# A fused attention and state-space layer: splits one tile per dense slice, a skip added in PSUM, a third result buffer

## The chip, the cores and the metric

One NeuronCore of a Trainium2 chip runs the whole layer as one program. The metric is the device time of one execution in microseconds (us). Engines are named as the profile names them: PE multiplies matrices (PEld loads its weights), DVE, ACT and POOL are the vector, scalar and general engines, and SP issues DMA transfers. PE writes its results to PSUM, in banks of 128 x 512 float32; the other tiles lie in SBUF.

## The reference

One layer over 1024 positions of 1024 channels, in float32. A combined projection feeds a sparse attention and a state-space (SSD) mixer; both are projected back, gated, merged, and followed by a SwiGLU block. What the change touches is the mixer's scan, its gate and norm, and the projections of both branches:

```python
    CB = jnp.einsum('bclgn,bcsgn->bcgls', Cc, Bc)
    y_diag = jnp.einsum('bcgls,bcgrls,bcsgrp->bclgrp', CB, Lmat, X)
    ...
    y_off = jnp.einsum('bclgn,bcgrpn,bcgrl->bclgrp', Cc, prev, jnp.exp(a_cum))
    y = (y_diag + y_off).reshape(Bsz, L, SSD_HEADS, SSD_HEADDIM) + d_skip[:, None] * xh
    y = y.reshape(Bsz, L, D_INNER)
    return rmsnorm(y * jax.nn.silu(z), ssd_norm)
```

`d_skip * xh` is D's skip. `Lmat` holds the exponentials of the decay between two positions of a chunk.

## The kernel before

Activations lie transposed, channels on partitions. Dense matrices keep float32 accuracy by three matmuls on two halves: a tile is split into a rounded "hi" (written by ACT) and the rest "lo" (written by DVE or POOL). For weights these are `whi` and `wlo` (L158, L159), for the attention's output `ath` and `atl` (L1299, L1303), for the mixer's output `yh` and `yw` (L1277, L1278).

The mixer works in 32 units, unit n = 4g + c for 8 head groups g and 4 chunks c of 256 positions. A unit has two generators. `ssd_in` loads `ld` (L1163, L1164) and the decay table `al` (L1169). ACT makes relu and exponentials of two tiles, the late part `M` and `al` (L1174 to L1176); PE multiplies B and C into `pcb`; DVE masks it to `cbm` (L1182) and multiplies it into `M` and `al` (L1184); X and the state's factors follow. `ssd_out` runs one unit later: PE's `pyd` (L1224, the part inside the chunk, which needs `al`) and `pyo` (L1234, the part from the state, absent for c = 0). DVE multiplies the decay `d_ea`, which was loaded into the result tile (L1218), by pyo (L1236), adds pyd (L1237), and adds D's skip for two tiles (L1241). For c = 0 ACT copies pyd in place of the first two (L1239). POOL multiplies by the gate z (L1243), SP stores to `d_y` (L1244), and ACT squares the result into `ysqt` (L1247) for the norm's sums on DVE (L1254).

Between these steps PE runs slices of dense work, six matmuls each, from the generator `beside`: the last gate projections (`pw`, `gate_run`), and the attention's output projection (`poa`, `poa_run`). The same generator splits what they need: `at_split` splits four tiles of the attention's output at once, and `y_load` loads and splits the first twelve tiles of the mixer's y for the projection `pos` (L1647), which follows the mixer.

The order on PE is the order in which the program is written (`in_order`). The order on ACT, DVE, POOL and SP is set by a scheduler from its own simulated times, when the program is built; added "behind" dependencies keep an instruction after another of the same engine. `exps[0]` names the two exponentials of the unit last begun, and `ysqt` is kept behind one of them. Each engine takes its queue strictly in order. DMAs from SP go round eight lanes, whose semaphores are DMAHW0 to DMAHW7, and each waits for the one eight before it.

The result tile, with z in one half and y in the other, comes from `vt` (one buffer) for every third unit and otherwise from the ring "R", which also serves `ld` and `al`. A load into a tile waits until its last use is over, for a result tile the store to `d_y`.

Of the kernel before, what the change touches and what calls it, by code (L numbers as in the profile page):

```python
# [10 lines left out]
F32 = mybir.dt.float32  # L11
F32R = mybir.dt.float32r
BF = mybir.dt.bfloat16
AF = mybir.ActivationFunctionType
OP = mybir.AluOpType
AX = mybir.AxisListType

P = 128
# [3 lines left out]
NT = L // P  # L22
# [17 lines left out]
POA_BOTH = 5  # L40
# [3 lines left out]
SK = 8  # L44
# [25 lines left out]
def build(tc, a, dbg=None, stop=99, slots=None):  # L70
    nc = tc.nc
    V, S, G, T, SP = nc.vector, nc.scalar, nc.gpsimd, nc.tensor, nc.sync
# [5 lines left out]
    wp = ctx.enter_context(tc.tile_pool(name="wp", bufs=2))  # L78
    vp = ctx.enter_context(tc.tile_pool(name="vp", bufs=1))
    H_ = Arena(ctx, tc, "H", n_slots["H"], 512)  # L80
    Q = Arena(ctx, tc, "Q", n_slots["Q"], 512)
    R = Arena(ctx, tc, "R", n_slots["R"], 1024)
# [105 lines left out]
    def col(name, j=0, n=1):  # L188
        o, _ = COLS[name]
        return vec[:, o + j:o + j + n]  # L190
# [6 lines left out]
    dsk = con.tile([P, 16], F32, name="dsk")  # L197
# [957 lines left out]
    exps = [None]  # L1155
# [51 lines left out]
    def ssd_out(c, g, z):  # L1207
        hs = slice(4 * g, 4 * g + 4)
        cl = slice(QC * c, QC * c + QC)
        X, M, xs, CT = z["X"], z["M"], z["xs"], z["bc"][:, 1]  # L1210
        st = state[:, g]
        zy = (vp.tile([P, NT, P], F32, name="vt", bufs=1).rearrange("p (j x) n -> p j (x n)", j=4) if (4 * g + c) % 3 == 0
              else R("zy", (P, 4, 256)))
        zc, yt = zy[:, 0:2], zy[:, 2:4]
        SP.dma_start(zc, d_z[2 * g:2 * g + 2].rearrange("j p l -> p j l")[:, :, cl])
        if c:
            for e in range(2):
                SP.dma_start(yt[64 * e:64 * e + 64],  # L1218
                             d_ea[c, hs].rearrange("(j e) l -> e j l", e=2)[e:e + 1].to_broadcast([64, 2, QC]))
        pyd = bank("pyd")  # L1220
        for j in range(2):
            for e in range(2):
                o = pyd[64 * e:64 * e + 64, 256 * j:256 * j + 256]
                T.matmul(o, X[:, 0, 2 * j + e], M[j][:, e], start=True, stop=False, skip_group_check=True)  # L1224
                T.matmul(o[:, 128:256], X[:, 1, 2 * j + e], M[2][:, 2 * j + e], start=False, stop=True, skip_group_check=True)
        if c < NCH - 1:
            pst = bank("pst")
            for t in range(2):
                T.matmul(pst[:, 0:256], z["bn"][:, t], z["Xd"][:, t].rearrange("p h n -> p (h n)"), start=t == 0, stop=t == 1)
        yield  # L1230
        if c:
            pyo = bank("pyo")
            for j in range(2):
                T.matmul(pyo[:, 256 * j:256 * j + 256], st[:, 128 * j:128 * j + 128], CT, start=True, stop=True)  # L1234
            ytf = yt.rearrange("p j l -> p (j l)")
            V.tensor_tensor(ytf, ytf, pyo, op=OP.mult)  # L1236
            V.tensor_tensor(ytf, ytf, pyd, op=OP.add)  # L1237
        else:
            S.activation(yt.rearrange("p j l -> p (j l)"), pyd, AF.Copy)  # L1239
        for j in range(2):  # L1240
            V.scalar_tensor_tensor(yt[:, j, :], xs[:, j], dsk[:, 2 * g + j:2 * g + j + 1], yt[:, j, :],  # L1241
                                   op0=OP.mult, op1=OP.add)
        G.tensor_tensor(yt, yt, zc, op=OP.mult)  # L1243
        SP.dma_start(d_y[2 * g:2 * g + 2].rearrange("j p l -> p j l")[:, :, cl], yt)  # L1244
        yield
        sq = Q("ysqt", (P, 2, 256))
        tc.add_manual_dep(S.activation(sq, yt, AF.Square).ins, exps[0][1], mybir.DependencyInfo(  # L1247
            mybir.DependencyClass.NoSync, mybir.DependencyReason.DATA), reason="behind")
        for j in range(2):
            ya_ = ysq[c // 2][:, QC * (c % 2):QC * (c % 2) + QC]  # L1250
            if g == 0 and j == 0:
                S.activation(ya_, sq[:, j], AF.Copy)
            else:
                V.tensor_tensor(ya_, ya_, sq[:, j], op=OP.add)  # L1254
        if c == 0:
            S.activation(st, pst[:, 0:256], AF.Copy)
        elif c < NCH - 1:
            G.tensor_tensor(st.rearrange("p (h n) -> p h n", h=4), st.rearrange("p (h n) -> p h n", h=4),
                            cdec[:, c, hs, None].to_broadcast([P, 4, 64]), op=OP.mult)
            V.tensor_tensor(st, st, pst[:, 0:256], op=OP.add)  # L1260
        yield
# [3 lines left out]
    def y_raw(k, b):  # L1265
        t = EV("yl")
        SP.dma_start(t, d_y[k][:, half(b)])
        return t

    def y_parts(i, j, src, where, scale=None, eng=V):  # L1270

        hi, lo = where("yh", dt=F32R), where("yw", dt=F32R)
        if scale is None:
            ins = S.activation(hi, src, AF.Copy)
            eng.tensor_tensor(lo, src, f(hi), op=OP.subtract)
        else:
            ins = S.activation(hi, src, AF.Copy, scale=scale)  # L1277
            V.scalar_tensor_tensor(lo, src, scale, f(hi), op0=OP.mult, op1=OP.subtract)  # L1278
        YO[i][j] = hi, lo
        return ins.ins  # L1280

    def y_load(ks, places):
        for k in ks:
            y_parts(1 + k // SK, k % SK, y_raw(k, 0), places(k), col("ssd_norm", k))

    def beside():

        AT = [([None, None], [None, None]) for _ in range(KT)]

        def at_load(b, ks, where):  # L1290
            raws = [EV("atl") for k in ks]
            for t, k in zip(raws, ks):
                SP.dma_start(t, d_att[k][:, half(b)])
            return b, ks, where, raws

        def at_split(b, ks, where, raws):
            for t, k in zip(raws, ks):
                hi, lo = where("ath", dt=F32R), where("atl", dt=F32R)
                i = S.activation(hi, t, AF.Copy).ins  # L1299
                for j in (ahead[0], *exps[0]):  # L1300
                    tc.add_manual_dep(i, j, mybir.DependencyInfo(
                        mybir.DependencyClass.NoSync, mybir.DependencyReason.DATA), reason="behind")
                (G if k % 2 else V).tensor_tensor(lo, t, f(hi), op=OP.subtract)  # L1303
                AT[k][0][b], AT[k][1][b] = hi, lo

        ahead = [None]

        def anchor(ins):
            ahead[0] = ins.ins.name

        def gate_run(t, b, w):
            p = bank_d("pw")
            yield from dense_steps(p, b, w, Hs)
            g = EV("g")
            anchor(S.activation(g, p, AF.Tanh, scale=0.5))
            SP.dma_start(d_gb[t][:, half(b)], g)
            yield

        def poa_run(t, b, w):
            ya = EV("ya")  # L1320
            SP.dma_start(ya, d_sga[t][:, half(b)])
            p = bank_d("poa")
            yield from dense_steps(p, b, w, AT)
            i = V.scalar_tensor_tensor(ya, ya, 1.0, p, op0=OP.add, op1=OP.mult)
            SP.dma_start(d_ya[t][:, half(b)], ya)
            yield

        def two_tiles(src, ts):
            W.plan(col_tile(src[ts[0]]) + col_tile(src[ts[1]])[:1])
            return [wpieces(ks8), [(W.next(), 0, ks8[:4]), (small_weights(src[ts[1]][:, 4:8]), 0, ks8[4:])]]  # L1330

        for t in range(6):
            yield from gate_steps(57 + t, d_gb[t])
        ld = at_load(0, range(AT_IN_Q), Q)
        w = two_tiles([a["w_in"][57 + t] for t in range(8)], (6, 7))
        yield from gate_run(6, 0, w[0])
        at_split(*ld)
        ld = at_load(0, range(AT_IN_Q, KT), H_)
        yield from gate_run(7, 0, w[1])
        at_split(*ld)  # L1340
        ld = at_load(1, range(4), H_)
        yield from gate_run(6, 1, w[0])
        at_split(*ld)
        ld = at_load(1, range(4, KT), H_)
        yield from gate_run(7, 1, w[1])
        w = two_tiles(a["w_o_attn"], (0, 1))
        yield from poa_run(0, 0, w[0])
        at_split(*ld)
        yield from poa_run(1, 0, w[1])
        for i in range(2):  # L1350
            yield from poa_run(i, 1, w[i])
        for ts, bs in [((t,), BS) for t in range(2, POA_BOTH)] + [(range(POA_BOTH, 8), (b,)) for b in BS]:
            for t in ts:
                W.plan(col_tile(a["w_o_attn"][t]))
                w = wpieces(ks8)
                for b in bs:
                    yield from poa_run(t, b, w)
            if bs == (0,):
                y_load(range(12), y_place)

    def y_place(k):
        return Q if k in Y_IN_Q else H_
# [801 lines left out]
```

## Time and profile before

| | us |
|---|---|
| median of three runs | 2359.83 (2356.86 to 2364.58) |
| profiled execution | 2361.0 |
| its span, first to last instruction | 2359.2 |
| mean granted clock of PE | 0.992 of full speed |
| PE busy | 2308.6 |
| DVE, ACT, POOL busy | 1658.4, 1220.9, 988.0 |
| the mixer's units | about 1118 to 1450 |
| step to the projection of y | about 1440 to 1500 |

Times within the span count from its start. Rows of the timeline give start, duration, engine, line, operation, out<-in, and in brackets how long the engine was idle before and which instruction ended that. Rows of waits give the total, the number of times and the longest. The granted clock is the share of full speed that PE was allowed.

### The profile page before, as it was taken

How to read it: one execution, taken by the hardware profiler on the slowest of the kernel's cores; microseconds unless marked ns; L12 is line 12 of the kernel's file. 1: busy time of each engine (PE TensorE's matmuls, PEld its weight loads, DVE VectorE, ACT ScalarE, POOL GpSimd, SP SyncE). 2: the span in 40 equal slices, each digit the busy share in tenths (PEclk: the TensorE clock that was granted, in tenths of full speed). 3: DMA queues.
4: the chain of work that ended last, by engine and by line, in shares of the span. 5: the costliest groups of instructions: out<-in, count | busy, mean ns of one | idle time of the engine just before them, and what ended most of it. 6: DMA issues, size and time to landing. Idle time of an engine off the chain costs nothing.

```text
span 2359.2 us, 35056 instructions
## 1 busy us (share of the span) xinstructions
PE 2308.6 (98%) x11736; PEld 1889.5 (80%) x11736; DVE 1658.4 (70%) x3185; ACT 1220.9 (52%) x2362; POOL 988.0 (42%) x787
## 2 busy tenths in 40 slices
PE   8999999999999999999999989999999999999997
PEld 5878888888888888887887777878788888888887
DVE  5467887499676767776678769865868776646675
ACT  4346666467645555556667565444555222235542
POOL 1435552522245656554445443000113445554556
PEclk8999999999999999999999999999999999999999
DMA  7137542622233433344679888864483444428664
GB/s 271 63 122 246 191 175 94 192 94 94 103 110 118 140 128 128 126 139 154 215 238 291 250 272 277 278 202 143 144 277 138 151 149 154 158 96 285 209 189 168
DMA packets 251716, 411.27 MB, mean 174 GB/s; under 512 B 25568, under 2 KB 93328, under 8 KB 251536
## 3 DMA queue, kind: packets, MB, share of 16 engines
q1 hardware_dynamic: 238288, 387.48, 49.2%
q10 hardware_dynamic: 13248, 21.56, 3.0%
q8 instruction: 92, 1.51, 0.3%
q14 instruction: 88, 0.72, 0.1%
HBM read 304.84 MB, written 107.24 MB: 175 GB/s over the span
## 4 chain that ended last, share of the span: by engine, by line
PE 74%; DVE 11%; DMA 7%; ACT 3%; issue 2%; POOL 1%; SPq 1%; DVEq 0%; ACTq 0%; POOLq 0%
PE p L1723 18%; PE pw L234 14%; PE pfo L1988 8%; PE pw L244 7%; PE plg L847 4%; PE pos L1647 3%; PE pot L1435 3%; PE prel L648 3%; PE pt L880 3%; PE po L896 3%; DVE junk L702 2%; PE puq L234 2%; DMA yl<-d_y 2%; PE poa L244 2%; DMA d_y<-zy 1%
## 5 line engine op out<-in xcount | busy, mean ns | idle before, releaser
L159 POOL TENSOR_TENSOR wlo<-wraw,whi 128x512 fp32r<-128x512 f32 x152 | 210.4, 1385 | 334.0 <-ACT whi L158 307.7
L1723 PE MATMUL p<-xh,wr 128*128 128x512 f32 x880 | 271.8, 389 | 0.0
L158 ACT ACTIVATE whi<-wraw 128x512 fp32r<-128x512 f32 x238 | 149.1, 627 | 214.0 <-issue 57.4
L1723 PEld LDWEIGHTS p<-xh,wr 128*128 128x128 f32 x880 | 165.2, 188 | 34.3
L1717 POOL TENSOR_TENSOR wr<-a,wr 128x512 fp32r<-128x512 f32 x82 | 115.2, 1413 | 134.0 <-ACT wr L1716 97.8
L1723 PE MATMUL p<-xl,wr 128*128 128x512 f32 x440 | 171.2, 389 | 0.0
L255 POOL TENSOR_TENSOR fwl<-fw,fwh 128x512 fp32r<-128x512 f32 (+1 forms) x78 | 106.7, 1377 | 104.0 <-ACT fwh L254 78.9
L1716 ACT ACTIVATE wr<-a 128x512 fp32r<-128x512 f32 x107 | 66.6, 629 | 127.5 <-PE p L1723 90.7
L859 ACT ACTIVATE lg<-lg,mx 128x256 f32<-128x256 f32 (+7 forms) x128 | 99.1, 774 | 58.3 <-DVE mx L856 50.8
L273 POOL TENSOR_TENSOR r<-v,nhalf 128x4 f32<-128x4 f32 (+1 forms) x17 | 20.0, 1178 | 260.7 <-DVE v L271 260.7
L654 DVE SCALAR_TENSOR_TENSOR acc<-rel,widx,acc 128x384 f32<-128x384 f32 (+2 forms) x90 | 102.9, 1168 | 15.8 <-ACT rel L649 15.6
L329 POOL TENSOR_TENSOR adaw<-adaw,cs 128x512 f32<-128x512 f32 x64 | 68.3, 1068 | 103.2 <-DMA adaw<-ada_w 93.1
L1723 PE MATMUL p<-h2h,wr 128*128 128x512 f32 x352 | 110.0, 390 | 0.0
L704 ACT ACTIVATE junk<-acc,cand__2216 128x1024 bf16<-128x1024 f32 (+2 forms) x96 | 86.2, 898 | 39.6 <-DVE cand__2216 L747 30.7
L649 ACT ACTIVATE rel<-prel 128x512 f32<-128x512 f32 (+3 forms) x160 | 76.9, 523 | 46.5 <-PE prel L648 43.3
L1723 PEld LDWEIGHTS p<-xl,wr 128*128 128x128 f32 x440 | 82.6, 188 | 17.1
L1647 PE MATMUL pos<-yh,wlo 128*128 128x512 f32 x224 | 87.9, 392 | 3.7 <-DVE wlo L159 2.3
L702 DVE TENSOR_SCALAR_CACHE_REDUCE junk<-acc,cand__2225 128x896 bf16<-128x896 f32 (+2 forms) x96 | 88.5, 922 | 1.5
L856 DVE CUSTOM_DVE_ANT_0 lg<-plg,nm 128x256 f32<-128x256 f32 (+1 forms) x128 | 51.5, 404 | 52.8 <-PE plg L847 52.1
L1647 PE MATMUL pos<-yh,whi 128*128 128x512 f32 x224 | 88.0, 393 | 0.5 <-ACT whi L158 0.4
L1717 POOL TENSOR_TENSOR wr<-s,wr 128x512 fp32r<-128x512 f32 x40 | 56.1, 1402 | 76.4 <-ACT wr L1716 69.2
L1647 PE MATMUL pos<-yw,whi 128*128 128x512 f32 x224 | 87.3, 390 | 0.0
(693 smaller groups left out, 7446.2 us busy)
## 6 DMA issues: line engine op xcount, KB each, us to landing
wraw<-w_in SPq DMA_DIRECT2D x129, 256.0 KB, 2.7
a<-w_ffn_in SPq DMA_DIRECT2D x122, 256.0 KB, 3.3
al<-d_a SPq DMA_DIRECT2D x88, 256.0 KB, 4.2
yl<-d_y SPq DMA_DIRECT2D x72, 256.0 KB, 4.6
adaw<-ada_w SPq DMA_DIRECT2D x64, 256.0 KB, 3.0
al<-d_ac SPq DMA_DIRECT2D x32, 512.0 KB, 5.2
d_a<-g SPq DMA_DIRECT2D x42, 256.0 KB, 2.4
ada<-ada_p SPq DMA_DIRECT2D x16, 512.0 KB, 7.6
```

What stands on the lines that cost most here:

```text
L158: self.hi = behind(S.activation(hi[:, :kt], raw[:, :kt], AF.Copy))
L159: self.lo = behind(self.eng[len(self.tiles) % len(self.eng)].tensor_tensor(lo[:, :kt], raw[:, :kt], f(hi[:, :kt]), op=OP.subtract))
L234: T.matmul(o, wt[:, k0 + i, :], xs[k][xi][b][:, sl], start=pi == 0 and i == 0 and wt is hi and xi == 0, stop=pi == len(pcs) - 1 and i == l ...
L244: T.matmul(o, wt[:, k0 + j, :], xs[k][xi][b], start=i == 0, stop=i == 23)
L255: (lo_eng or V).tensor_tensor(lo, src, f(hi), op=OP.subtract)
L654: V.scalar_tensor_tensor(acc[i][:, 0:n], rel[:, 0:n], ws, acc[i][:, 0:n], op0=OP.mult, op1=OP.add)
L702: V.tensor_scalar(jk, y, a_, 0.0, op0=op, op1=OP.add, accum_out=o)
L859: S.activation(lg[:, 0:n], lg[:, 0:n], AF.Exp, scale=-1.0, bias=m, accum_out=rr[:, 2 * t + hh:2 * t + hh + 1])
L1647: T.matmul(p, w[k // 4][wi][:, k % 4], YO[i][k][xi], start=start and k == 0 and n == 0, stop=k == SK - 1 and n == 2, skip_group_check=True)
L1717: parts_last[0] = parts_eng[0].tensor_tensor(w[:, 1], src, f(w[:, 0]), op=OP.subtract).ins.name
L1723: T.matmul(p, w[:, wi, i], X[x][i][xi], start=start and i == 0 and k == 0, stop=i == 3 and k == 2, skip_group_check=True)
L1988: T.matmul(p, w[wi][:, k - k0], xs[k][xi][:, sl], start=start and k == 0 and i == 0, stop=k == KH - 1 and i == 2, skip_group_check=True)
```

## The change

Four edits. (1) D's skip is added to pyd in PSUM, as soon as pyd is there, and after pyo only two instructions remain on DVE; for c = 0 the skip writes the result tile from pyd itself, and ACT's copy goes. (2) A third result buffer: where n % 3 is 1, z and y are two tiles of an earlier stage's tag `adaw`, and the ring "R" is left out. (3) `at_split` returns jobs, one tile each, which `along` runs one per dense slice. (4) `y_load` too returns one job per tile, loads up to two tiles ahead, and its `yh` is kept behind the exponentials of the unit last begun; the twelve jobs run along the last six `poa_run`s (2, 1, 1, then 4, 2, 2), where they stood together after the third of these.

```diff
-        zy = (vp.tile([P, NT, P], F32, name="vt", bufs=1).rearrange("p (j x) n -> p j (x n)", j=4) if (4 * g + c) % 3 == 0
-              else R("zy", (P, 4, 256)))
-        zc, yt = zy[:, 0:2], zy[:, 2:4]
+        if (4 * g + c) % 3 == 1:
+            zcf, ytf = (wp.tile([P, 4, P], F32, name="zy", tag="adaw", bufs=2).rearrange("p k m -> p (k m)") for _ in range(2))
+        else:
+            zy = (vp.tile([P, NT, P], F32, name="vt", bufs=1).rearrange("p k m -> p (k m)") if (4 * g + c) % 3 == 0 else R("zy"))
+            zcf, ytf = zy[:, 0:512], zy[:, 512:1024]
+        zc, yt = (x.rearrange("p (j l) -> p j l", j=2) for x in (zcf, ytf))
...
-            ytf = yt.rearrange("p j l -> p (j l)")
             V.tensor_tensor(ytf, ytf, pyo, op=OP.mult)
+        for j in range(2):
+            py = pyd[:, 256 * j:256 * j + 256]
+            V.scalar_tensor_tensor(py if c else yt[:, j], xs[:, j], dsk[:, 2 * g + j:2 * g + j + 1], py,
+                                   op0=OP.mult, op1=OP.add)
+        if c:
             V.tensor_tensor(ytf, ytf, pyd, op=OP.add)
-        else:
-            S.activation(yt.rearrange("p j l -> p (j l)"), pyd, AF.Copy)
-        for j in range(2):
-            V.scalar_tensor_tensor(yt[:, j, :], xs[:, j], dsk[:, 2 * g + j:2 * g + j + 1], yt[:, j, :],
-                                   op0=OP.mult, op1=OP.add)
...
-    def y_load(ks, places):
-        for k in ks:
-            y_parts(1 + k // SK, k % SK, y_raw(k, 0), places(k), col("ssd_norm", k))
+    def y_load(ks, places, tie):
+
+        raws = {}
+
+        def load(k):
+            if k in ks:
+                raws[k] = y_raw(k, 0)
+
+        def one(k):
+            for x in range(k, k + 3):
+                if x not in raws:
+                    load(x)
+            tie(y_parts(1 + k // SK, k % SK, raws[k], places(k), col("ssd_norm", k)))
+
+        return [lambda k=k: one(k) for k in ks]
...
+            return [lambda t=t, k=k: one(t, k) for t, k in zip(raws, ks)]
+
+        def behind_exps(i):
+            for j in (ahead[0], *exps[0]):
+                tc.add_manual_dep(i, j, mybir.DependencyInfo(
+                    mybir.DependencyClass.NoSync, mybir.DependencyReason.DATA), reason="behind")
+
+        def along(run, jobs):
+
+            jobs = list(jobs)
+            for _ in run:
+                if jobs:
+                    jobs.pop(0)()
+                yield
+            for job in jobs:
+                job()
...
-        at_split(*ld)
+        jobs = at_split(*ld)
         ld = at_load(0, range(AT_IN_Q, KT), H_)
-        yield from gate_run(7, 0, w[1])
+        yield from along(gate_run(7, 0, w[1]), jobs)
...
+        y_jobs = y_load(range(12), y_place, behind_exps)
...
-                    yield from poa_run(t, b, w)
-            if bs == (0,):
-                y_load(range(12), y_place)
+                    n = len(bs) == 1 and ((2, 1, 1), (4, 2, 2))[b][t - POA_BOTH]
+                    yield from along(poa_run(t, b, w), [y_jobs.pop(0) for _ in range(n)])
```

The order on PE is the same in both kernels. On the other engines it differs from about 1100 us of the profile until about 1550, where both run alike again. Three places follow. In the rows, the number behind a name tells buffers apart, "waits" lists the semaphores that an instruction waits for, and their suffix is a mere number.

First ACT at unit 24 before the change. Its tiles are `al_13922` and `M_13924`; `al_14014` belongs to unit 25.

```order
L1201 ACTIVATE bn_13967<-pbn_13964 128x256
L1175 ACTIVATE al_13922<-al_13922,acum_941 128x256 x4
L1176 ACTIVATE M_13924<-M_13924 128x512
L1277 ACTIVATE yh_14732<-yl_14730,vec_87 128x512
L1176 ACTIVATE al_13922<-al_13922 128x1024
L158 ACTIVATE whi_14241<-wraw_14240 128x512
L1247 ACTIVATE ysqt_14007<-zy_13977 128x512
```

The first split of y stands between the two exponentials of the unit. After the change, with unit 24's tiles `al_13924` and `M_13926`:

```order
L1201 ACTIVATE bn_13969<-pbn_13966 128x256
L1175 ACTIVATE al_13924<-al_13924,acum_941 128x256 x4
L1176 ACTIVATE M_13926<-M_13926 128x512
L1176 ACTIVATE al_13924<-al_13924 128x1024
L158 ACTIVATE whi_14243<-wraw_14242 128x512
L1249 ACTIVATE ysqt_14009<-zy_13979 128x512
```

The split has left this place: the first one now follows the exponentials of unit 29.

Second, ACT at unit 17 before, with the tiles `al_13230` and `M_13232`; `M_13336` is unit 18's.

```order
L1176 ACTIVATE M_13232<-M_13232 128x512
L174 ACTIVATE uh_13382<-uraw_13381 128x512
L1315 ACTIVATE g_13353<-pw_13267 128x512
L1247 ACTIVATE ysqt_13326<-zy_13301 128x512
L1174 ACTIVATE M_13336<-al_13334,acum_941 128x128 x4
L1176 ACTIVATE al_13230<-al_13230 128x1024
L1299 ACTIVATE ath_13243<-atl_13144 128x512
```

Four instructions, relu of the next unit among them, stand between the exponentials. After the change, with `al_13231` and `M_13233`:

```order
L1176 ACTIVATE M_13233<-M_13233 128x512
L1258 ACTIVATE state_11603<-pst_13306 128x256
L1176 ACTIVATE al_13231<-al_13231 128x1024
L1314 ACTIVATE ath_13259<-atl_13129 128x512
L174 ACTIVATE uh_13383<-uraw_13382 128x512
L1249 ACTIVATE ysqt_13323<-zy_13295 128x512
```

One copy of the state is left between them; the other instructions come later. On DVE at the same place the product of `al` (L1184) stood behind the two `ysq` of `ysqt_13326`, and it now stands ahead of them.

Third, SP at the loads of unit 24 before. `zy_13696` is the result tile of an earlier unit, and DMAHW6 in the fourth row is the lane of its store.

```order
L1244 DMA d_y_108<-zy_13696 128x2x256 [waits Pool_49]
L157 DMA wraw_14460<-w_o_attn 128x512 [waits DMAHW7_49,Pool_49]
L1325 DMA d_ya_104<-ya_13715 128x512 [waits DMAHW0_49,DVE_49]
L1163 DMA ld_13919<-d_bc_106 128x2x256 [waits DMAHW6_49,DMAHW1_49,Activation_49]
L1164 DMA ld_13919<-d_xs_107 128x2x256 [waits DMAHW2_49]
L1169 DMA al_13922<-d_ac_113 128x1024 [waits DMAHW3_49,PE_49]
```

The load of `ld` waits for the store three rows earlier, whose slot it takes. After the change, `zy_13881` and `zy_13882` are the two tiles of the new buffer for unit 22:

```order
L1246 DMA d_y_108<-zy_13615 128x2x256 [waits DMAHW6_49,Pool_49]
L1218 DMA zy_13881<-d_z_105 128x2x256 [waits DMAHW7_49]
L1221 DMA zy_13882<-d_ea_114 64x2x256 [waits DMAHW6_49,DMAHW0_49,Activation_49]
L1354 DMA d_ya_104<-ya_13605 128x512 [waits DMAHW1_49,DVE_49]
L1169 DMA al_13842<-d_ac_113 128x1024 [waits DMAHW2_49,PE_49]
L1221 DMA zy_13882<-d_ea_114 64x2x256 [waits DMAHW3_49]
L1163 DMA ld_13921<-d_bc_106 128x2x256 [waits DMAHW4_49,DVE_49]
L1164 DMA ld_13921<-d_xs_107 128x2x256 [waits DMAHW5_49]
```

The load of `ld` for unit 24 no longer waits for a store. The first load of `d_ea` into the new buffer does, for the store two rows above it, and the load of unit 23's `al` stands behind it.

More of the change, by code (lines that the diff above doesn't have):

```diff
@@ L1296, in at_split, with one @@
         def at_split(b, ks, where, raws):
-            for t, k in zip(raws, ks):
+            def one(t, k):
                 hi, lo = where("ath", dt=F32R), where("atl", dt=F32R)
[L1299 to L1302, printed above, removed]
+                behind_exps(S.activation(hi, t, AF.Copy).ins)
                 (G if k % 2 else V).tensor_tensor(lo, t, f(hi), op=OP.subtract)
                 AT[k][0][b], AT[k][1][b] = hi, lo
+            return [lambda t=t, k=k: one(t, k) for t, k in zip(raws, ks)]
[11 more added lines that the diff above has]
+                job()
         ahead = [None]
@@ L1336, in beside @@
         yield from gate_run(6, 0, w[0])
-        at_split(*ld)
+        jobs = at_split(*ld)
         ld = at_load(0, range(AT_IN_Q, KT), H_)
-        yield from gate_run(7, 0, w[1])
-        at_split(*ld)
+        yield from along(gate_run(7, 0, w[1]), jobs)
+        jobs = at_split(*ld)
         ld = at_load(1, range(4), H_)
-        yield from gate_run(6, 1, w[0])
-        at_split(*ld)
+        yield from along(gate_run(6, 1, w[0]), jobs)
+        jobs = at_split(*ld)
         ld = at_load(1, range(4, KT), H_)
-        yield from gate_run(7, 1, w[1])
+        yield from along(gate_run(7, 1, w[1]), jobs)
+        jobs = at_split(*ld)
         w = two_tiles(a["w_o_attn"], (0, 1))
-        yield from poa_run(0, 0, w[0])
-        at_split(*ld)
+        yield from along(poa_run(0, 0, w[0]), jobs)
         yield from poa_run(1, 0, w[1])
```

## The prediction

> **What bounds the kernel now.** I read the engines' busy times first, then the table by stage, then what TensorE waits for.
>
> ```profile
> PE 2308.6 (98%) x11736; PEld 1889.5 (80%) x11736; DVE 1658.4 (70%) x3185; ACT 1220.9 (52%) x2362; POOL 988.0 (42%) x787
> ```
>
> TensorE (PE) is busy for 98% of the span. The change alters neither its instructions nor their order, so it can only alter PE's idle time and the clock. Both are found by stage, over the mixer (about 1118 to 1450 us) and the step out of it:
>
> ```profile
> 1280.00:1320.00 40.00, 35.36 (x190) 27.82 (x190) 33.06 (x46) 26.11 (x59) 21.36 (x17) 0.96 0.85 279
> 1320.00:1360.00 40.00, 36.63 (x210) 28.99 (x206) 26.34 (x43) 21.96 (x51) 15.70 (x13) 1.00 0.81 239
> 1360.00:1400.00 40.00, 34.01 (x184) 27.09 (x185) 27.28 (x44) 26.20 (x57) 14.24 (x11) 0.87 0.85 276
> 1400.00:1440.00 40.00, 40.00 (x223) 32.23 (x223) 33.60 (x47) 26.62 (x55) 21.96 (x17) 1.00 0.77 238
> 1440.00:1480.00 40.00, 36.15 (x163) 27.93 (x162) 38.34 (x55) 23.14 (x41) 10.29 (x7) 1.00 0.95 320
> 1480.00:1520.00 40.00, 38.69 (x172) 31.46 (x171) 39.80 (x66) 20.77 (x37) 2.65 (x1) 1.00 0.91 295
> ```
>
> The columns are the stretch, its length, busy PE, weight loads, DVE, ACT and POOL, then PE's granted clock and the DMA share. Three stretches of the mixer hold idle PE and two a lower clock. After 1440 it is DVE that has almost nothing left: it idles 1.9 of 80 us. What PE waits for from 1110 to 1620:
>
> ```profile
> PE pyd L1224 <- DVE al L1184: 11.1, 3, 7.1
> PE pcb L1179 <- DMA ld<-d_bc: 2.9, 2, 2.3
> PE pos L1647 <- DVE wlo L159: 2.3, 3, 1.0
> ```
>
> The first two rows are the mixer's: 14.0 us. The large ones stand alone, each at one place, and two are followed by a slow clock:
>
> ```profile
> 1289.47 0.66 PE L1224 MATMUL pyd<-al,X 128*64 128x256 f32 x4 [3.36 <-DVE al L1184]
> 1346.32 0.67 PE L1179 MATMUL pcb<-ld 128*128 128x256 f32 x2 [2.28 <-DMA ld<-d_bc]
> 1365.99 1.13 PE L1224 MATMUL pyd<-al,X 128*64 128x256 f32 x4 [7.08 <-DVE al L1184]
> 1290.00:1294.00 4.00, 4.00 (x21) 3.05 (x18) 2.09 (x4) 3.56 (x7) 1.63 (x2) 0.57 0.98 295
> 1366.00:1372.00 6.00, 6.00 (x24) 4.46 (x25) 3.89 (x7) 3.66 (x10) 3.23 (x3) 0.51 0.93 298
> ```
>
> The lost clock is 4 x 0.43 = 1.7 us behind the gap of 3.36, and 6 x 0.49 = 2.9 us behind that of 7.08. The gap of 2.28 costs none (clock 1.00 in its stretch). So the whole mixer loses 14.0 + 1.7 + 2.9 = 18.6 us: no more than this can be had there.
>
> **The change, part by part.** First the y splits, at unit 24 (ACT, then DVE, then SP's issues):
>
> ```profile
> 1354.60 0.62 ACT L1176 ACTIVATE M<-M 128x512 f32<-128x512 f32 x1
> 1362.92 0.72 ACT L1277 ACTIVATE yh<-yl,vec 128x512 fp32r<-128x512 f32 x1 [7.70 <-DMA yl<-d_y]
> 1363.55 1.04 ACT L1176 ACTIVATE al<-al 128x1024 f32<-128x1024 f32 x1
> 1357.61 0.88 DVE L1241 SCALAR_TENSOR_TENSOR zy<-ld,dsk,zy 128x256 f32<-128x256 f32 x2
> 1363.67 0.75 DVE L1278 SCALAR_TENSOR_TENSOR yw<-yl,vec,yh 128x512 fp32r<-128x512 f32 x1 [5.18 <-ACT yh L1277]
> 1364.62 1.23 DVE L1184 TENSOR_TENSOR al<-al,cbm 128x1024 f32<-128x1024 f32 x1 [0.20 <-ACT al L1176]
> 1359.22 0.32 SPq L1267 DMA_DIRECT2D yl<-d_y  x1
> ```
>
> ACT is ready for al's exponential at 1355.2, but the queue holds the first yh ahead of it, and that waits 7.70 us for a load issued only at 1359.22. Behind the exponential stand DVE's product and PE's pyd. In the changed order the exponential follows M's directly. DVE then sets the time: even if both D's skip instructions stay ahead, it is free at 1358.49, and pyd follows the product's start by 1365.99 - 1364.62 = 1.37 us, so at 1359.9. PE ran dry at 1365.99 - 7.08 = 1358.91, so 0.9 us are left, and no slow clock. Gain: 6.1 + 2.9 = 9.0 us. The changed order also puts the skip ahead of pyo's product, where DVE waits; then some 0.1 us are left, and I take 9.3. Its bounds are 10.0 (all) and 6 (a wait of 2 to 3 us by another late load, clock kept).
>
> [...]
>
> Next the attention splits, at unit 17:
>
> ```profile
> 1283.89 0.62 ACT L1176 ACTIVATE M<-M 128x512 f32<-128x512 f32 x1
> ...
> 1285.93 1.27 ACT L1174 ACTIVATE M<-al,acum 128x128 f32<-128x128 f32 x4
> 1287.10 1.05 ACT L1176 ACTIVATE al<-al 128x1024 f32<-128x1024 f32 x1
> 1286.07 1.99 DVE L1254 TENSOR_TENSOR ysq<-ysq,ysqt 128x256 f32<-128x256 f32 x2
> 1288.19 1.23 DVE L1184 TENSOR_TENSOR al<-al,cbm 128x1024 f32<-128x1024 f32 x1
> ```
>
> Here four instructions (uh, g, ysqt and the next unit's M) stand between the two exponentials, and DVE runs both ysq before the product. Afterwards only a state copy stands between, and the product stands ahead of the two ysq. The exponential could start at about 1284.7, end at 1285.7, and pyd follow 1.28 us later (1289.47 - 1288.19), at 1287.0. PE ran dry at 1286.11, so 0.9 of 3.36 stays and the clock holds: gain 2.5 + 1.7 = 4.2. Bounds: 5.1 (all) and 0 (ACT has an equal backlog elsewhere, since every split is still made). I take 4.1.
>
> The third gap, of 2.28 us, comes from ld's first load, which waited on SP for a y store that frees its slot. In the changed order that load waits for no store, but the next al load does. I take half of the 2.9 us of ld waits, 1.4, between 0 and 2.9.
>
> D's skip in PSUM, and ACT's copies for c = 0, which go:
>
> ```profile
> L1241 DVE SCALAR_TENSOR_TENSOR zy<-ld,dsk,zy x42: 469/479/1559, 1145.8 to 1447.2; 128x256 f32<-128x256 f32 x42
> L1239 ACT ACTIVATE zy<-pyd 128x512 f32<-128x512 f32 x5 | 2.9, 583 | 1.1 <-PE pyd L1225 1.1
> L2010 DVE SCALAR_TENSOR_TENSOR aq<-aq,gf,prn 128x256 f32<-128x256 f32 x16 | 6.4, 477 | 4.8 <-PE prn L279 4.8
> 1429.64 1.91 DVE L1241 SCALAR_TENSOR_TENSOR vt<-ld,dsk,vt 128x256 f32<-128x256 f32 x2
> ```
>
> Eight copies of 0.583 us leave ACT: 4.7 us. DVE's 64 instructions stay. None of this shape writes PSUM in the trace; the nearest, with one input from PSUM, takes 0.477 on the mean, like the median of 0.479 here. Ends: 0.47 and 1.56 each; I take 0.48, by which the slow pair of 1.91 becomes 0.9. After pyo two instructions are left in place of four, so y is done 0.9 us earlier (the usual pair), 1.9 in the slow pair. PE waits for none of it, since y goes to POOL, a store and ysqt; those have a whole unit, (1450 - 1118) / 32 = 10.4 us. I book 0 in the mixer. If the cover goes (ysqt is late ahead of the next relu), it is worth at most the gaps left above, 0.9 us each.
>
> [...]
>
> The third result buffer frees slots of the ring "R": seven allocations for three units, not eight. It removes waits on SP and adds others:
>
> ```profile
> SPq L1215 <- DMA d_y<-vt: 22.8, 9, 6.0
> SPq L1169 <- DMA d_y<-zy: 21.5, 10, 4.5
> al<-d_ac SPq DMA_DIRECT2D x31, 512.0 KB, 5.4
> ```
>
> Of 32 units, about 19 have an ld or al load that waits for a y store, and afterwards about 10: nine waits of some 2.2 us less (21.5 / 10). The new buffer's d_ea load waits at seven places for the unit's own store, one to three instructions earlier, with the next al load behind it: 7 x 2.5 (22.8 / 9) = 17 us. SP stands about as long as before, but at other places, so I add a loss: one new gap like the 2.28 and one of 0.7, 3 us; bounds 0 and 18 (below).
>
> The end of the stage. Before, four y tiles are split inside the units and eight behind the last exponentials; now all twelve come behind unit 29 or later.
>
> ```profile
> L1278 DVE SCALAR_TENSOR_TENSOR yw<-yl,vec,yh 128x512 fp32r<-128x512 f32 x17 | 15.9, 957 | 8.9 <-ACT yh L1277 8.9
> ```
>
> Four yw move towards the place where DVE is full: 4 x 0.75 (the undisturbed one above) = 3.0 us, less the 1.0 us that the slow skip pair gives back there, leaves 2.0; four of the 256 KB loads move too. Half of that reaches PE, which waits 2.3 us for DVE's wlo now: loss 1, bounds a gain of 1 (the skip alone counts) and a loss of 7 (rival A).
>
> Sum: -9.3 - 4.1 - 1.4 + 0 + 3 + 1 = -10.8 us. The profiled execution took 2361.0, so 2350.2; the median of the runs is 2359.83, 1.2 lower, which gives 2349.
>
> **The rivals.** What this kernel's measurement can tell from no change is about 0.3%, 7.1 us: faster lies below 2352.8, slower above 2366.9.
>
> A, the end takes it back. Twelve splits and their loads come late, while DVE idles 1.9 of 80 us and DMA stands at 0.95. Four yw at the mean of 0.957 are 3.8 us, and four loads of 262 KB at that stretch's 320 GB/s are 3.3 us, both ahead of the first dense tile of the next stage. That is a loss of 7 in place of 1: 2355. For it: no slack on DVE. Against: from 1400 to 1440 DVE has 6.4 us and ACT 13 us free, and eight splits stood there before without any gap.
>
> B, slower: SP is held at the new d_ea loads. For unit 24, SP and ACT show:
>
> ```profile
> 1344.44 0.42 SPq L1169 DMA_DIRECT2D al<-d_ac  x1
> 1351.86 0.97 ACT L1174 ACTIVATE M<-al,acum 128x128 f32<-128x128 f32 x3
> ```
>
> Its al load was issued 7.4 us before relu began; 5.4 of them are landing, so 2.0 us are slack. The waits for a store reach 6.0 us. Where one exceeds 2.0 with al behind, relu, the exponentials and pyd start late. A gap of 7.08 with its clock costs 10.0 us: two such, less the 3 us already in the sum, give 2349 + 17 = 2366, and with a short one of 2.3 us 2368. It decides from two gaps long enough to lower the clock. Against it: SP waits now as often for the same stores, and al's loads cause no listed PE gap.
>
> C, all gaps close, with nothing new: 2361.0 - 18.6 - 1.2 = 2341. For it: ACT is 52% busy and DVE 70%, so the gaps are matters of order. Against: the order is made anew, and five gaps in 32 units were left in the one before.
>
> D, the change does not do what it says: at unit 24 pyd would have waited anyway, for the d_ea load of the unit ahead, since its product with pyo is ahead of al on DVE:
>
> ```profile
> 1355.09 0.69 DVE L1236 TENSOR_TENSOR zy<-zy,pyo 128x512 f32<-128x512 f32 x1 [2.36 <-DMA ld<-d_xs]
> ```
>
> It waited 2.36 us for a load even there. With another 2.5 us (the mean wait of such a load for a store) on the 0.9 left, the gap is 3.4 with a slow clock of 1.7: a gain of 10.0 - 5.1 = 4.9. With no gain at unit 17 the sum is -4.9 - 1.4 + 3 + 1 = -2.3: 2357. Against: the product ran 3.8 us before PE ran dry.
>
> **How the numbers follow.** Forecast 0.50, with its own range 2344 to 2354, of which 0.42 below 2352.8 and 0.08 above; A 0.15 and D 0.08, both no difference; C 0.12, faster; B 0.15, slower. So faster 0.54, same 0.31, slower 0.15. Leaving out half of B above and a little below C gives 2340 to 2367.
>
> **What would show it.** Right: no pyd gap above 3 us and a clock of 1.00 in every stretch from 1118 to 1440; yh behind the last units' exponentials, no ACT wait for a y load in the units before; no ACT copy of pyd; every skip instruction at about 0.48 us. Wrong: relu waiting for an al load behind a d_ea load on SP (B); PE idle above 6 us from 1440 to 1520 with DVE's wlo as the releaser, or waiting for a y half (A); a long wait of DVE at pyo's product for d_ea (D). The prediction is wrong outright if the time is lost outside the mixer, whose order it takes to be unchanged elsewhere.

## The result and the profile after

The changed kernel takes 2373.77 us (six runs, 2368.53 to 2375.50) against 2359.47 before (2355.32 to 2364.58). The ratio is 1.0056, with a 95% interval of 1.0040 to 1.0073: it is slower by 14 us, where 11 us less were forecast, and it lies above the stated range. The profiled execution spans 2372.1 us, 12.9 more than before.

The engines' busy times of the changed kernel:

```profile
PE 2311.1 (97%) x11736; PEld 1891.8 (80%) x11736; DVE 1645.6 (69%) x3185; ACT 1216.0 (51%) x2354; POOL 980.3 (41%) x787
```

DVE, ACT and POOL all do less work than before (DVE 12.8 us less). The time is in PE's idle stretches and its clock again. By stage, with the columns as before:

```profile
1280.00:1320.00 40.00, 35.43 (x200) 28.28 (x199) 30.62 (x46) 25.11 (x58) 22.44 (x18) 0.96 0.94 294
1320.00:1360.00 40.00, 37.93 (x216) 30.15 (x215) 27.13 (x45) 23.33 (x53) 16.68 (x14) 1.00 0.71 217
1360.00:1400.00 40.00, 35.15 (x183) 27.30 (x182) 20.02 (x36) 19.75 (x48) 10.37 (x9) 0.91 0.73 234
1400.00:1440.00 40.00, 37.19 (x201) 29.47 (x200) 32.79 (x48) 26.46 (x55) 19.04 (x16) 0.96 0.74 219
1440.00:1480.00 40.00, 29.28 (x115) 22.16 (x113) 25.98 (x37) 17.05 (x29) 9.75 (x8) 0.87 0.80 263
```

Idle PE is now spread over the mixer, and the worst stretch is the step out of it, where PE is busy 29.3 of 40 us. PE's waits from 1110 to 1620 (the lines after 1209 have moved by a few: pyd is L1227 here, D's skip is still L1241, pyo's product is L1238, pyd's addition L1244, the store L1246, a y load L1269):

```profile
PE poa L244 <- ACT whi L158: 8.1, 1, 8.1
PE pyd L1227 <- DVE al L1184: 6.3, 4, 2.8
PE pos L1676 <- DVE wlo L159: 3.1, 5, 1.4
PE pcb L1179 <- DMA ld<-d_bc: 3.0, 2, 2.1
PE prn L279 <- POOL r L273: 2.6, 1, 2.6
PE pcb L1179 <- DVE cbm L1182: 2.6, 1, 2.6
PE pbn L1199 <- DVE zy L1238: 2.0, 1, 2.0
```

The 11.1 us of pyd behind al are down to 6.3, none longer than 2.8: the gaps of 7.1 and 3.4 us are gone. In their place stand one gap of 8.1 us at the end of the stage and six of 1.8 to 2.8 us. Idle PE and lost clock (the share below full speed, while PE is busy) from 1110 to 1600 add up to 25.7 us before and 40.4 now. Cut at the end of the mixer's last pyd (about 1435 in both), this is 18.7 us in the mixer and 7.0 behind it before, and 22.5 and 17.9 now: most of the added loss appears behind the mixer.

Ahead of most of these gaps a load comes late, and SP, which issues the loads, stands longer for stores. First the waits of SP in the mixer, then those of ACT, now and before:

```profile
SPq L1218 <- DMA d_y<-vt: 39.6, 10, 5.9
SPq L1221 <- DMA d_y<-zy: 29.8, 7, 6.0
SPq L1169 <- DMA d_y<-zy: 25.1, 8, 5.5
```

```profile
ACT M L1174 <- DMA al<-d_ac: 22.8, 8, 8.5
ACT M L1174 <- DMA al<-d_ac: 3.2, 2, 2.3
```

L1218 loads z, L1221 `d_ea`, L1169 al. With 2.0 us in another row, SP stands 96.5 us for y stores, where it stood 72.9 (23.1 + 22.8 + 21.5 + 5.5). The number of such waits is nearly the same, 26 now and 27 before; each is longer, 3.7 us on the mean and not 2.7. So al's loads are late: relu waits 22.8 us for them (3.2 before). Measured from the issue of an al load to the relu that uses it, unit by unit, the median lead is 8.1 us, before 12.6. An al load landed 5.4 us after its issue in the trace before (median), so little is left. Two places on SP, and the relu that the second delays:

```profile
1326.39 0.47 SPq L1246 DMA_DIRECT2D d_y<-zy  x1
1326.91 0.47 SPq L1218 DMA_DIRECT2D zy<-d_z  x1
1332.93 0.58 SPq L1221 DMA_DIRECT2D zy<-d_ea  x1
...
1357.54 0.42 SPq L1354 DMA_DIRECT2D d_ya<-ya  x1
1364.66 0.33 SPq L1269 DMA_DIRECT2D yl<-d_y  x1
1365.09 0.39 SPq L1246 DMA_DIRECT2D d_y<-zy  x1
1365.52 0.46 SPq L1218 DMA_DIRECT2D zy<-d_z  x1
1366.08 0.50 SPq L157 DMA_DIRECT2D wraw<-w_o_attn  x1
1368.46 1.23 SPq L1221 DMA_DIRECT2D zy<-d_ea  x2
1369.78 0.54 SPq L1169 DMA_DIRECT2D al<-d_ac  x1
```

```profile
1375.01 1.28 ACT L1174 ACTIVATE M<-al,acum 128x128 f32<-128x128 f32 x4 [8.51 <-DMA al<-d_ac]
```

At both places a load that needs a store's buffer is the next or second next row after that store, and SP stands until the store has landed: 5.6 us from the end of one issue to the next behind 1326.91, 6.7 behind 1357.54 (there a y load behind a store to d_ya, in the ring EV). Whatever follows waits with it; the al load of 1369.78 lands 8.5 us after ACT was ready for it.

The end of the stage, SP first, then ACT and PE:

```profile
1437.88 0.42 SPq L1354 DMA_DIRECT2D d_ya<-ya  x1
1438.35 0.49 SPq L1246 DMA_DIRECT2D d_y<-vt  x1
1443.98 0.32 SPq L1269 DMA_DIRECT2D yl<-d_y  x1
```

```profile
1454.68 0.72 ACT L1594 ACTIVATE yl<-yl,vec 128x512 f32<-128x512 f32 x1 [11.29 <-DMA yl<-d_y]
1455.31 0.61 ACT L158 ACTIVATE whi<-wraw 128x512 fp32r<-128x512 f32 x1
```

```profile
1455.97 0.79 PE L244 MATMUL poa<-ath,whi 128*128 128x512 f32 x1 [8.08 <-ACT whi L158]
```

The y load of 1443.98 waited 5.1 us for the store to d_ya two rows above it, and with it the loads of the next stage. ACT's queue holds the next stage's first scaling of y (L1594) ahead of a whi that PE needs, so PE stood 8.1 us and the clock fell: 1440 to 1480 at 0.87.

### The profile page after: what moved, and what is told of

Its sections match the earlier page's. It is cut to its first block, busy times and chain, and to the rows that moved or that the text cites. A ratio compares the mean times of both kernels' runs of the same rounds, so it can differ in the third digit from the quotient of the medians.

```text
span 2372.1 us, 35062 instructions
## 1 busy us (share of the span) xinstructions
PE 2311.1 (97%) x11736; PEld 1891.8 (80%) x11736; DVE 1645.6 (69%) x3185; ACT 1216.0 (51%) x2354; POOL 980.3 (41%) x787
## 5 line engine op out<-in xcount | busy, mean ns | idle before, releaser
L273 POOL TENSOR_TENSOR r<-v,nhalf 128x4 f32<-128x4 f32 (+1 forms) x17 | 18.2, 1070 | 263.8 <-DVE v L271 263.8
L1752 PEld LDWEIGHTS p<-xl,wr 128*128 128x128 f32 x440 | 82.6, 188 | 17.2
```

Of the source, the lines that this page charges most:

```text
L1752: T.matmul(p, w[:, wi, i], X[x][i][xi], start=start and i == 0 and k == 0, stop=i == 3 and k == 2, skip_group_check=True)
```

## Experiments

All ratios are to the kernel before, run on the same chip in the same round; e1 to e4, e5 to e8, e9 to e12 and e13 to e15 ran on four chips. "SP" is SP's wait for y stores from 1110 to 1445, "lead" the median time from an al load's issue to its relu, "lost" PE's idle time and lost clock from 1110 to 1600, first in the mixer (up to the last pyd), then behind it. These three come from one profiled execution each, whose time can lie several us from the median; e15's was 10 us above it, with the excess outside this window.

| kernel | edits | ratio (95%) | SP us | lead us | lost us, mixer + behind |
|---|---|---|---|---|---|
| before | none | 1 | 72.9 | 12.6 | 18.7 + 7.0 |
| changed | 1 2 3 4 | 1.0056 (1.0040 to 1.0073) | 96.5 | 8.1 | 22.5 + 17.9 |
| e5 | 1 | 1.0085 (1.0062 to 1.0109) | 110.6 | 9.1 | 34.9 + 6.2 |
| e3 | 2 | 0.9978 (0.9964 to 0.9992) | 63.3 | 15.4 | 12.9 + 7.7 |
| e6 | 3 | 1.0003 (0.9991 to 1.0016) | 77.9 | 12.0 | 19.7 + 6.7 |
| e1 | 4 | 1.0004 (0.9993 to 1.0014) | 78.4 | 11.5 | 14.5 + 18.0 |
| e2 | 1 2 3 | 1.0042 (1.0027 to 1.0057) | 95.9 | 9.9 | 29.1 + 8.1 |
| e8 | 1 2 4 | 1.0056 (1.0037 to 1.0076) | 101.8 | 8.2 | 14.7 + 19.9 |
| e7 | 2 3 4 | 0.9969 (0.9956 to 0.9982) | 66.2 | 14.5 | 7.0 + 14.5 |
| e4 | all, y loads in own tiles | 1.0069 (1.0046 to 1.0092) | 83.3 | 9.9 | 26.9 + 15.2 |
| e9 | 1, late | 1.0014 (1.0000 to 1.0029) | 91.8 | 10.9 | 18.2 + 12.2 |
| e10 | all, 1 late | 0.9993 (0.9982 to 1.0005) | 73.8 | 11.4 | 11.6 + 15.4 |
| e11 | all, y stores from ACT | 0.9982 (0.9972 to 0.9991) | 57.4 | 14.7 | 11.1 + 8.0 |
| e12 | 2 3 4, scalings late | 0.9958 (0.9943 to 0.9973) | 69.2 | 15.1 | 8.3 + 6.6 |
| e13 | none, y stores from ACT | 1.0002 (0.9992 to 1.0013) | 63.8 | 13.8 | 18.2 + 8.2 |
| e14 | all, stores from ACT, scalings late | 0.9957 (0.9941 to 0.9973) | 57.0 | 15.2 | 11.0 + 5.0 |
| e15 | 2 3 4, scalings late, stores from ACT | 0.9963 (0.9949 to 0.9976) | 66.3 | 17.2 | 9.0 + 7.4 |

**First theory: the y loads (edit 4), against the result buffer (edit 2).** The trace after shows y loads that stand on SP for a store to d_ya, so edit (4) was the first suspect.

Edit (4) alone (e1), as in the diff of the change:

> The kernel before with edit (4) alone: the twelve splits of y one per dense slice, behind the exponentials. Theory S (slots): the loads of y take slots of the ring EV that they share with the attention's results ya; each waits some 5 us on SP for a store to d_ya, and the al load behind it comes late. Then this edit alone takes away the gap of 7.1 us at unit 24 and adds waits of SP for d_ya stores (about 20 us from 1110 to 1430, against 9.4 before) and a long PE gap with slow clock at 1450: 2366 to 2374 us. Rival B (the d_ea loads of the new result buffer hold SP): the buffer is not in it, so only the gain at unit 24 is left, 2346 to 2353. Rival O (any new order of the queues is worth several us either way): anything from 2350 to 2370, with gaps whose releasers are not al loads behind y loads.

2362.23 us, no difference, which lies in the range of rival O alone. The gap at 1456 has its twin here, 6.0 us at 1444, and a yh no longer stands ahead of unit 24's exponential. The edit gives back at the end what it gains in the middle (18.0 us lost behind the mixer for 7.0, 14.5 in it for 18.7); it does not make the loss.

All but edit (4) (e2): the three others with the old `y_load`.

> The changed kernel without edit (4): the splits of y stand together after the third poa_run, not tied to the exponentials, as before. Theory S: the waits of SP for d_ya stores go back to about 10 us and the 8 us gap at 1456 goes, while the 7 us gap at a yh of units 24 to 26 can return: 2352 to 2362. Rival B: SP is still held at d_ea, the loss stays: 2366 to 2376. Rival O: 2350 to 2370 without relation to either wait.

2370.50 us: the loss stays without it. The first theory falls. Here the old yh gap came back at 14.3 us, since the y load stood behind a d_ya store and ACT behind the y load.

Edit (2) alone (e3):

> The kernel before with edit (2) alone, the third result buffer. Theory S: SP's waits only change places, 2355 to 2364, the yh gap of 7 us still there. Rival B: relu waits over 15 us for al loads (3.2 before) and PE gains new gaps of over 2.5 us: 2365 to 2376. Rival O: within 8 us of 2359, other gaps.

2355.36 us: faster by 0.22%. Rival B falls as well. SP stands less (63.3 us), no relu waits for al, and the lead grows to 15.4 us.

Own tiles for the y loads (e4):

```diff
-                raws[k] = y_raw(k, 0)
+                raws[k] = wp.tile([P, 4, P], F32, name="yl", tag=("uraw", "uh", "ul")[k % 3], bufs=1).rearrange("p k m -> p (k m)")
+                SP.dma_start(raws[k], d_y[k][:, half(0)])
```

> The changed kernel, but the first twelve y loads go into three tiles that the stage does not use (the tags uraw, uh, ul), so none of them waits for a store to d_ya. Theory S: SP's wait of these loads for d_ya stores is zero, al comes in time, the gap of 8 us at 1456 is gone or below 3: 2345 to 2357. Rival B: only the part of the loss at the end goes, relu still waits over 15 us for al: 2360 to 2368. Rival O: 2350 to 2372, with gaps elsewhere.

2376.90 us, no better, and above all three ranges. The first y loads wait for no store, but the next users of the ring EV do (ya loads and the next stage's y loads), and one of these scalings held ACT for 12.2 us.

**Second round: which edit.** Each of the other two alone, and each left out.

D's skip in PSUM alone (e5):

> The kernel before with edit (1) alone, D's skip added in PSUM. Theory H (the skip stands at the head of DVE's queue and waits for pyd; M's and al's products stand behind it): DVE waits 8 to 14 us for pyd, as in the slow kernels so far, and the time is 2364 to 2374. Theory O (each edit makes the scheduler deal the loads on SP anew, and what counts is which loads come to stand right behind a store whose buffer they take): SP's order changes little here, so 2354 to 2364, with the gap of 7 us at a yh still there.

2377.81 us: this edit alone is slower than all four, and slower than theory H had it. DVE waits 14.2 us for pyd, as theory H said, but PE's new gaps have another releaser. The waits of PE, the waits of SP (the last row is from the kernel before), and one of the gaps with the SP rows ahead of it:

```profile
PE pyd L1224 <- DVE al L1184: 11.2, 3, 8.7
PE pcb L1179 <- DMA ld<-d_bc: 10.1, 4, 3.5
PE px L1190 <- DMA ld<-d_xs: 2.4, 2, 1.3
```

```profile
SPq L1163 <- DMA d_y<-zy: 57.6, 15, 6.1
SPq L1215 <- DMA d_y<-vt: 41.0, 9, 6.6
SPq L1163 <- DMA d_y<-zy: 23.1, 7, 5.8
```

```profile
1320.47 0.38 SPq L1244 DMA_DIRECT2D d_y<-vt  x1
1320.95 0.41 SPq L1325 DMA_DIRECT2D d_ya<-ya  x1
1321.48 0.70 SPq L1321 DMA_DIRECT2D ya<-d_sga  x1
1326.17 0.37 SPq L1215 DMA_DIRECT2D vt<-d_z  x1
1326.88 0.58 SPq L1218 DMA_DIRECT2D vt<-d_ea  x1
1327.55 0.54 SPq L1163 DMA_DIRECT2D ld<-d_bc  x1
```

```profile
1331.68 0.89 PE L1179 MATMUL pcb<-ld 128*128 128x256 f32 x2 [3.39 <-DMA ld<-d_bc]
```

PE waits 12.5 us for loads of ld, 2.9 before. SP's waits for a y store ahead of an ld load went from 23.1 to 57.6 us, those of z's loads into `vt` from 22.8 to 41.0. In the rows shown, the load of z into `vt` stands for the store of `vt` three rows above it, 4.0 us after the row ahead ended, and the ld load that PE needs is issued behind it. Two more of the four gaps at pcb, at 1236 and 1363, have the same order ahead of them. The old gap at unit 24 stays, 8.7 us in place of 7.1, again at a yh. SP does not stand longer at the stores themselves: it waits 6.6 us there for POOL, 8.1 before.

Edit (3) alone (e6):

> The kernel before with edit (3) alone, the attention's splits one per slice. Theory H: no wait of DVE for pyd, 2352 to 2360. Theory P (the spread splits themselves cause the gaps of 1.5 to 2.6 us between 1270 and 1310 that the slow kernels share): these gaps are here, 2362 to 2370. Theory O: no relation, 2352 to 2372.

2359.18 us, no difference and in theory H's range; theory P (the spread splits) falls. The gap at unit 17 is 2.4 us here, but another of 3.2 us came.

All but the skip (e7). L1241 to L1244 of the changed kernel are as before:

> The changed kernel without edit (1): the skip follows pyo's products again, ACT's copies are back. Theory H: the loss in the mixer goes, 2352 to 2361. Theory P: the gaps from 1270 to 1310 stay, 2366 to 2374. Theory O: anything from 2352 to 2374; the time follows the waits of SP for stores.

2350.45 us, faster by 0.31% (0.18 to 0.44) and a little below theory H's range. All but edit (3) (e8):

> The changed kernel without edit (3): four splits of the attention's output at once again. Theory H: still slow, 2366 to 2376. Theory P: the gaps from 1270 to 1310 go, 2355 to 2364. Theory O: anything from 2352 to 2374, by SP's waits for stores.

2370.01 us. Of the kernels so far, each with the early skip is slower by 0.42 to 0.85%, and each without it is at par or faster. The skip costs 20 us both alone (1.0085) and on top of the other three (1.0056 - 0.9969 = 0.0087). The traces tell it apart from edit (4) by place: the skip adds 16 us of lost time in the mixer both times (18.7 to 34.9, and 7.0 to 22.5), while edit (4) moves loss behind it (14.5 to 19.9 us in the four kernels of the first two rounds that have it and the old loads, 6.2 to 8.1 in the others).

**Third round: why the skip costs.** The instructions themselves are not slow: none of the 64 takes over 0.491 us, the 48 that write PSUM 0.488 in the median.

```profile
L1241 DVE SCALAR_TENSOR_TENSOR pyd<-ld,dsk,pyd x48: 475/488/491, 1138.0 to 1442.2; 128x256 f32<-128x256 f32 x48
```

What differs is SP's order. Take every ld, al or z load that waits for a y store, and count how many rows it stands behind that store. Before, 2 of 27 stand in the very next row, and 8 one or two rows behind. With the skip alone it is 11 and 16 of 28. In the changed kernel 6 stand in the next row, without the skip (e7) 1. A load in the next row waits 5.7 us on the mean with the skip alone, one three rows behind 3.6. Theory R: with pyo's chain shorter, the scheduler counts on an earlier store, and puts the load that takes its buffer right behind it; on the chip a y store lands 5.0 us (before) to 6.3 us (skip alone) after its issue in the median, so SP stands longer, and later loads are issued later. To test it, the place was given back and PSUM kept (e9, and e10 with all edits):

```diff
-            V.tensor_tensor(ytf, ytf, pyo, op=OP.mult)
+            off = V.tensor_tensor(ytf, ytf, pyo, op=OP.mult).ins.name
...
+            if c:
+                tc.add_manual_dep(i, off, mybir.DependencyInfo(
+                    mybir.DependencyClass.NoSync, mybir.DependencyReason.DATA), reason="behind")
```

Here `i` is the skip's instruction on pyd.

> The kernel before with edit (1) alone, but the skip's two instructions on pyd are kept behind pyo's product on DVE (for c above 0). PSUM is still written, only the place in the order is given back. Theory R (the early skip lets the scheduler place the y store earlier, and then the load that takes the store's buffer right behind it, where SP stands for the store's whole landing; in the order of skip alone 11 of 28 such loads stand one row behind the store, here 6, before 2): the loads are issued in time again, 2354 to 2364. Theory U (adding in PSUM itself costs): still 2370 to 2380.

> The changed kernel, all four edits, with the skip kept behind pyo's product in the same way. Theory R: like the changed kernel without the skip's edit, 2346 to 2356, with the al loads issued 12 us or more ahead of relu in the median (8 in the changed kernel). Theory U: 2366 to 2376.

2362.97 and 2356.06 us: of the 0.85% of the skip alone 0.14 is left, and the changed kernel goes from 1.0056 to 0.9993. Theory U (PSUM itself) falls for most of the cost: it is the place on DVE. The count of rows does not give the size, though: in e9 6 loads stand in the next row, as many as in the changed kernel, and SP still stands 91.8 us, with hardly any loss. That the cost depends on which load is late for PE fits these runs but is not shown. A rest of 0.24% against e7 stays. In e10 one new gap, with DVE's rows, shows where it can come from:

```profile
PE pyo L1237 <- DVE zy L1247: 5.2, 2, 4.7
```

```profile
1303.68 0.69 DVE L1356 SCALAR_TENSOR_TENSOR ya<-ya,poa 128x512 f32<-128x512 f32 x1 [4.38 <-DMA ya<-d_sga]
1304.29 1.29 DVE L1318 TENSOR_TENSOR atl<-atl,ath 128x512 fp32r<-128x512 f32 x2
1305.49 0.68 DVE L1247 TENSOR_TENSOR zy<-zy,pyd 128x512 f32<-128x512 f32 x1
```

PE's pyo waits for pyd's last addition (L1247 there), the last use of a bank of PSUM. It is now the last of four instructions, and other work came in between, here one that waits 4.4 us for a load. The lead came to 11.4 us and not the 12 expected.

Second test: the early skip stays, and the y stores go to ACT's queue, just ahead of ysqt (e11).

```diff
-        SP.dma_start(d_y[2 * g:2 * g + 2].rearrange("j p l -> p j l")[:, :, cl], yt)
+        tc.add_manual_dep(S.dma_start(d_y[2 * g:2 * g + 2].rearrange("j p l -> p j l")[:, :, cl], yt).ins, exps[0][1], mybir.DependencyInfo(
+            mybir.DependencyClass.NoSync, mybir.DependencyReason.DATA), reason="behind")
```

> The changed kernel, but the y stores are issued by ACT, just ahead of ysqt, which waits for the same product of POOL; the skip stays early on DVE. Theory R: SP no longer carries the stores, the loads wait for a store that was issued when its data was ready, and the loss shrinks: 2350 to 2364. Theory H (DVE standing at its head for pyd is the cost): DVE waits as long as before, 2368 to 2378. An equal loss could also come from 32 more issues on ACT.

2353.44 us: 0.9982, where the changed kernel stands at 1.0056. SP stands 57.4 us, and the lead is 14.7. DVE's wait for pyd in this run, and in e14, which has the stores on ACT too (below):

```profile
DVE pyd L1241 <- PE pyd L1228: 5.0, 7, 1.4
DVE pyd L1241 <- PE pyd L1228: 9.1, 11, 1.4
```

It was 10.5 us in 8 waits in the changed kernel. In e11 it is half of that; in e14 it is nearly as long, and e14 is faster than the kernel before. So DVE's standing for pyd is not what costs, and theory H as the main cause falls.

The control, the kernel before with its stores from ACT (e13):

> The kernel before, only with its y stores issued by ACT ahead of ysqt. If the early skip and the loads right behind the store are what the store from ACT cured (theory R), there is less to cure here: 2350 to 2360, a gain of at most half of the 20 us that it gave the changed kernel. If stores on SP cost any kernel as much (theory G), 2336 to 2346.

2359.35 us, no difference. The stores on SP cost little by themselves; the early skip made them dear. That is what theory R says and theory G denies. Theory O was right that SP's order counts, and wrong that any edit shifts it as much: each of the other three alone ends at par or faster.

**The end of the stage.** In e7 PE still stood 4.2 us at a whi behind a scaling of y that ACT held 11.5 us. There the first two scalings were kept behind the last whi of the mixer (e12):

```diff
-            S.activation(y21, y21, AF.Copy, scale=col("ssd_norm", k))
+            i = S.activation(y21, y21, AF.Copy, scale=col("ssd_norm", k)).ins
+            if k < 2:
+                tc.add_manual_dep(i, last_hi[0], mybir.DependencyInfo(
+                    mybir.DependencyClass.NoSync, mybir.DependencyReason.DATA), reason="behind")
```

> The changed kernel without edit (1), and the first two scalings of the next stage's y are kept behind the last weights' rounding (whi) on ACT. In the run without edit (1) PE stood 4.2 us at a whi behind such a scaling, with a slow clock, and 3.0 us at a wlo soon after. If the place in ACT's queue is the cause, these go: 2342 to 2348. If the y loads behind it are late anyway, the wait comes back at pos: 2349 to 2353.

2347.72 us, at the upper edge of what was expected: 0.42% below the kernel before (0.27 to 0.57). The same with all four edits and the stores from ACT (e14), and without the skip's edit but with the stores (e15):

> All four edits, the y stores from ACT, and the first two scalings of the next stage's y behind the last whi. The run with the stores from ACT still lost 8 us after the mixer, of them 3.1 and a slow clock at prn, none of it at that whi: so little is left to gain, 2348 to 2354.

> The changed kernel without the skip's edit, with the scalings behind the last whi, and the y stores from ACT. By theory R the loads are in time there already, so the stores change little: 2342 to 2350. By theory G another 10 us go: 2332 to 2340.

2349.76 and 2349.05 us. e12, e14 and e15 lie within each other's intervals; all three beat both kernels. e14 and e15 differ by edit (1) alone, 0.9957 and 0.9963: with the y stores out of SP's queue the early skip costs nothing, with them in it 20 us. With the stores and the scalings elsewhere, the four edits are 0.43% faster than the kernel before.

## Why the prediction was wrong

**The step that failed** is D's skip: "I book 0 in the mixer". It costs 20 us, 16 of them in the mixer by the traces. With 0 in its place the time is that of e7, 2350.45, inside the stated range. The prediction saw that y is done earlier, and took earlier as harmless because PE waits for none of it. It did not ask what an earlier y sets off: the store moves in SP's queue, and more of the loads that want its buffer come right behind it (6 in the next row, 2 before). The order was there to be read. The prediction counted how many loads wait for a store (19 of 32 units before, 10 after, and seven new ones) and priced each at the mean wait of before, 2.2 and 2.5 us. Those 6 wait 4.8 us on the mean, and the 11 of e5 5.7. Counting the rows would have shown the danger, but not its size, as e9 tells.

**The two large gaps** were read rightly. The yh left unit 24, the four splits left unit 17, and neither gap is in the trace after. Without the skip, the other edits give 8 us (e7), where the prediction's sum was 10.8. In e7 the mixer loses 11.7 us less than before, where the sum's terms for the mixer give 11.8; that is luck in part, since the buffer's term among them had the wrong sign.

**The result buffer** was a loss of 3 us in the sum and the mechanism of rival B. Alone it is a gain of 5 us (2360.43 - 2355.36). Rival B had the right queue, SP, the right victim, al's load, and the right slack (a lead with about 2 us to spare), but the wrong edit: the d_ea loads wait 18.4 us in e3 and 29.8 in the changed kernel, because the skip moved the stores there too. The relu that waits longest in the changed kernel, 8.5 us, has two waits of SP for a store ahead of it, 1.9 us at a `d_ea` load and 6.7 us at a y load of edit (4), for a store to `d_ya`.

**The end of the stage** is the second term that was mis-sized: a loss of 1, with rival A at 7. Behind the mixer idle time rose from 7.0 to 14.7 us, and 3.2 us of clock were lost: 10.9 us, and 7.5 even without the skip (e7). The cause was not DVE, as rival A had it, which had 14 us free from 1440 to 1480: it was ACT's order and the y loads on SP. With the two scalings moved on ACT (e12) 6.6 us are lost there, no more than before.

**D's skip instructions**, on the other hand, run as forecast at 0.48 us, with no slow pair left: none of the 64 takes over 0.491 us, where the longest before took 1.559 into `zy` and 1.575 into `vt` (L1241). What slowed those is not shown. They take 6 us of DVE less in all (30.2 us from 1110 to 1500, 36.5 before), which PE was not waiting for.

Shown: the skip's early place on DVE, together with the y stores in SP's queue, is the cause, since the loss goes when either is changed (e10, e11, e14 against e15). Not settled: that it is the loads in the next row which carry the loss is read from the counts, and e9 does not fit. Why the scheduler places the load there (theory R: it counts on an earlier landing than the chip's) is argued.

## What to carry to other kernels

Work that is finished earlier moves everything which a scheduler hangs on it; ask of each store which load takes its buffer, and how many rows of its queue lie between. A load right behind that store stops the whole queue until the store has landed, here for 5 to 6 us, and what can be lost is the loads behind it, which PE misses later and under another name. When edits are bundled, time each alone: here three were worth 8 us and the fourth cost 20.

## What was not expected of the hardware

PE's clock fell after shorter gaps than the trace before had shown. There, 2.28 us left it at full speed and 3.36 halved it, and the prediction took a wait of 2 to 3 us as one that keeps the clock. In the changed kernel 2.62 us (at 1304) and 2.81 (at 1404) were each followed by 3.4 us at half speed, as were 2.24 us in e1 (at 1317) and 1.87 in e2 (at 1349), while 2.42 and 2.85 us in e15 and 3.36 us in e3 (at 1285) were not. So between 1.9 and 3.4 us it went either way here; a gap that looks short enough can cost 1.7 us more.

What tells them apart is where a gap lies. From 1110 to 1610 the clock of each trace changes only at steps 3.41 us apart; in the changed kernel it falls at 1305.4, 1377.1, 1404.4 and 1452.2 and is back 1, 2, 1 and 3 steps later. All 17 traces together have 44 such steps at full speed with PE idle for over 2.0 us of the step, by its rows, and each was followed by half speed; of the 2364 with less than 1.85 us idle, 2 were. In e3 the edge of a step cuts the gap of 3.36 us into 1.37 and 1.99, and nothing follows.
